# Four rows of the first fourth chunk, loaded through ScalarE's DMA queue

## The chip, the cores and the metric

The kernel runs on one core of a Trainium2 chip. The metric is device time in microseconds (us) of one execution. Without the profiler, three runs of the kernel before took 1325.69, 1326.71 and 1327.58 us; their median, 1326.71 us, is the time before. One execution was profiled, and its trace is what every view below was read from.

## The reference

For two batches, eight heads and rows and columns of 2112, a bias that depends on the clipped distance of row and column is added to the logits, and a softmax is taken over each row:

```python
rel = pos[:, None] - pos[None, :]
rel_clipped = np.clip(rel, -max_rel, max_rel) + max_rel      # max_rel = 16
logits = logits + rel_bias[:, rel_clipped][None, :, :, :]
exp = np.exp(logits - logits.max(axis=-1, keepdims=True))
return (exp / exp.sum(axis=-1, keepdims=True)).astype(np.float32)
```

There are 2 x 8 x 2112 = 33,792 rows of 8,448 bytes. All of them are read once and written once.

## The kernel before, in words

The rows are laid over 128 partitions, 264 consecutive rows to a partition. They are worked off in 44 chunks; a chunk is 6 consecutive rows of every partition (`R = 6`), so 50,688 contiguous bytes in each partition and 6336 KB in all. Four chunks make one pass of the outer loop (`NBUF = 4`, 11 passes), and chunk number m of a pass lives in buffer `X[m]`. There are just these four buffers, so at any time at most four chunks are between the start of their load and the end of their store.

Who does what:

- SyncE issues the loads (`load`, line 89), all on its own DMA queue, which the page lists as q1. At the start it issues chunks 0 to 3 one behind the other (lines 95 and 96). Then it loops: it waits until the store of chunk n has landed (`take` on `st[m]`, line 86) and issues the load of chunk n + 4 into the same buffer.
- VectorE first builds the bias table (lines 118 to 166; the shuffle at line 142 is the first instruction there that needs `rel_bias` in SBUF). In each pass it copies a window of that table (line 170), and for each chunk it waits for the load (`take` on `ld[m]`, line 86), then adds the bias row by row while it takes the maximum (line 184, six instructions), waits for ScalarE's sums, takes their reciprocal (line 208) and scales four of the six rows (line 211).
- ScalarE takes the exponential of each row (line 195), scales the other two rows (line 216), waits until all six rows are scaled, and issues the store (`store`, line 93) on its own DMA queue, which the page lists as q10. Ahead of all that it issues the small load of `rel_bias` (line 120) on the same queue.

So the order of the transfers is set by two queues, each first in first out: SyncE's holds only loads of chunks, ScalarE's holds the small bias load and then only stores. A transfer of a whole chunk is 128 contiguous rows of 50,688 bytes, one for each partition; the 16 DMA engines take 8 of them each. "Row" below, when a DMA is meant, is one of these 50,688-byte rows.

Below, Ln and Sn are the load and the store of chunk n, counted from 0 to 43 over all passes.

Of the kernel before, what the change touches and what calls it, by code (L numbers as in the profile page):

```python
# [15 lines left out]
def kernel(  # L16
# [6 lines left out]
    nc = tc.nc  # L23
    P = 128
    B, H, S, S2 = logits.shape
# [3 lines left out]
    RP = B * H * S // P  # L29
# [4 lines left out]
    NBUF = 4  # L34
    R = 6
# [2 lines left out]
    assert K * G == RP  # L38
    SW = S + G - 1
    DV = 4  # L40

    io = ctx.enter_context(tc.tile_pool(name="io", bufs=1))
    X = [io.tile([P, R * S], FP32, tag=f"X{b}", name=f"X{b}") for b in range(NBUF)]
# [21 lines left out]
    def view(t, offset, dims):  # L65
        return bass.AP(tensor=t.tensor, offset=t.offset + offset, ap=[[list(t.ap[0])[0], P]] + dims)

    def rows(t, k, m):
        return bass.AP(
            tensor=t.tensor, offset=t.offset + m * R * S + k * (G * S), ap=[[RP * S, P], [1, R * S]],  # L70
        )

    with tc.tile_critical(no_gpsimd_drain=True):  # L73
        ld = [nc.alloc_semaphore(f"ld{b}") for b in range(NBUF)]
# [6 lines left out]
        zero = nc.alloc_semaphore("zero")  # L81
        idx = nc.alloc_semaphore("idx")
        dve = nc.alloc_semaphore("dve")

        def take(eng, sem, n):
            eng.wait_ge(sem, n).then_inc(sem, -n)  # L86

        def load(k, m):
            nc.sync.dma_start(out=X[m][:, :], in_=rows(logits, k, m)).then_inc(ld[m], 16)
# [2 lines left out]
            take(nc.scalar, scaled, R)  # L92
            nc.scalar.dma_start(out=rows(out, k, m), in_=X[m][:, :]).then_inc(st[m], 16)

        for m in range(NBUF):
            load(0, m)
        with nc.Fori(0, K - 1, 1, engines=[ENG.SP]) as k:
            for m in range(NBUF):
                take(nc.sync, st[m], 16)
                load(k + 1, m)  # L100
# [3 lines left out]
        v = nc.vector  # L104
# [6 lines left out]
        def settle():  # L111
# [9 lines left out]
            out=bass.AP(tensor=F2.tensor, offset=F2.offset, ap=[[Q * step, P // Q], [1, H * W]]),  # L121
            in_=bass.AP(tensor=rel_bias.tensor, offset=rel_bias.offset, ap=[[0, P // Q], [1, H * W]]),
        ).then_inc(rb, 16)
        nc.gpsimd.iota(pid[:, :], pattern=[[0, 2]], base=0, channel_multiplier=1).then_inc(idx, 1)
        nc.gpsimd.iota(
            num, pattern=[[1, NB + 1]], base=0, channel_multiplier=0,
# [11 lines left out]
        for o, n, s, op in ((eq, NB, q, ALU.is_equal), (lt, NB, q, ALU.is_lt), (hsel, NB, h, ALU.is_equal),  # L138
# [24 lines left out]
                           in_=view(reg, 1, [[1, NB - 1], [0, RP - W]])))  # L163
# [9 lines left out]
        def row(m, i):  # L173
            return X[m][:, i * S : (i + 1) * S]

        def col(t, m, i, n=1):
            c = m * R + i
            return t[:, c : c + n]

        def add(m):  # L180
            take(v, ld[m], 16)
            for i in range(R):
                x = G - 1 - m * R - i
                v.tensor_tensor_reduce(  # L184
                    out=row(m, i), in0=row(m, i), in1=F2[:, x : x + S],
                    scale=-1.0, scalar=BIG, op0=ALU.add, op1=ALU.min, accum_out=col(nmax, m, i),
                ).then_inc(added, 1)
# [12 lines left out]
        def scales_begin(eng, m):  # L200
            if m < NBUF - 1:
                eng.wait_ge(inv, m + 1)
            else:
                take(eng, inv, NBUF)

        def scale(m):
            take(v, expd, R)
            v.reciprocal(out=col(rec, m, 0, R), in_=col(tot, m, 0, R)).then_inc(inv, 1 if m < NBUF - 1 else NBUF + 1)  # L208
            scales_begin(v, m)
            for i in range(DV):  # L210
                v.tensor_scalar_mul(out=row(m, i), in0=row(m, i), scalar1=col(rec, m, i)).then_inc(scaled, 1)  # L211

        def scale_rest(m):
            scales_begin(nc.scalar, m)
            for i in range(DV, R):
                nc.scalar.activation(  # L216
# [3 lines left out]
        with nc.Fori(0, K, 1, engines=[ENG.DVE]) as k:  # L220
            window(k)
            for m in range(NBUF):
                add(m)
                scale(m)
# [36 lines left out]
```

## Time and profile before

| What | Value |
|---|---|
| median of 3 runs without profiler | 1326.71 us |
| profiled execution, its own time | 1327.36 us |
| its span in the trace | 1325.6 us |
| VectorE (DVE) busy | 866.1 us, 65% |
| ScalarE (ACT) busy | 757.2 us, 57% |
| DMA, bytes moved | 570.98 MB |

The span runs from the first to the last thing that the profile records of the execution; 1.8 us of the profiled execution's own time lie outside it. Busy shares are shares of the span. The profile's page gives for each engine the busy time, for the DMA the busy share in 40 equal slices of the span and the GB/s in each, and for each DMA instruction how long after its issue its data had landed. In the view in order of time, a row begins with the start and the duration in us, then engine, line and operation; "SPq" and "ACTq" are the parts of SyncE and ScalarE that issue DMAs and wait on semaphores. What stands in square brackets is the idle time of the engine just before the row, and what ended it. "DVEq L86" there is a wait of VectorE on a semaphore, line 86 being the helper that all such waits go through.

### The profile page before, as it was taken

To read this page: it belongs to the slowest core of one execution; us is meant where nothing else is said; L and a number is where in the kernel's file an instruction comes from. 1 tells how busy PE (TensorE), PEld (TensorE's weight loads), DVE (VectorE), ACT (ScalarE), POOL (GpSimd) and SP (SyncE) were. 2 spreads that over 40 slices of the span, in tenths; PEclk is the share of its full clock that TensorE was granted. 3 is DMA by queue.
4 is the path that set the end of the run, shared out by engine and by line. 5 is a ranking of instruction groups with operands and counts; after the bars stand their busy time and mean duration, and the time that the engine had idled before them with its cause. 6 is when DMAs were issued, how large, how long until landed. Compare 5 with 4: busy or idle time off the path is not lost. (4 is left out here: it accounts for less than half of the span.)

```text
span 1325.6 us, 2109 instructions
## 1 busy us (share of the span) xinstructions
DVE 866.1 (65%) x781; ACT 757.2 (57%) x627; POOL 0.4 (0%) x6
## 2 busy tenths in 40 slices
DVE  6886656566766675566667566556766676566663
ACT  3776555556665565555556565555665665555563
POOL 0000000000000000000000000000000000000000
DMA  9999999999999999999999999999999999999998
GB/s 416 416 433 424 441 428 428 441 424 433 441 428 431 436 425 433 439 430 434 434 430 433 437 434 425 437 434 434 428 439 436 422 441 434 431 431 436 428 433 389
DMA packets 12682, 570.98 MB, mean 431 GB/s; under 512 B 1412, under 2 KB 1416, under 8 KB 1416
## 3 DMA queue, kind: packets, MB, share of 16 engines
q1 hardware_dynamic: 6336, 285.48, 50.1%
q10 hardware_dynamic: 6344, 285.48, 49.8%
q14 instruction: 2, 0.02, 0.0%
HBM read 285.48 MB, written 285.47 MB: 431 GB/s over the span
## 5 line engine op out<-in xcount | busy, mean ns | idle before, releaser
L195 ACT ACTIVATE X<-X,nmax 128x2112 f32<-128x2112 f32 x264 | 542.6, 2055 | 508.0 <-DVE nmax L184 475.3
L184 DVE CUSTOM_DVE_ANT_0 X<-X,F 128x2112 f32<-128x2112 f32 x264 | 605.2, 2354 | 322.3 <-DVEq L86 322.3
L211 DVE TENSOR_SCALAR X<-X,rec 128x2112 f32<-128x2112 f32 x176 | 220.3, 1315 | 2.8
L216 ACT ACTIVATE X<-X,rec 128x2112 f32<-128x2112 f32 x88 | 176.1, 2048 | 17.2 <-DVE rec L208 12.2
L208 DVE RECIPROCAL rec<-tot 128x6 f32<-128x6 f32 x44 | 8.4, 191 | 106.2 <-DVEq L86 106.2
L195 ACT ACTIVATION_READ_ACCUMULATOR X<-X,nmax 128x1 f32 x264 | 49.2, 186 | 0.0
L195 ACT ACT_TABLE_LOAD x11 | 14.1, 1283 | 22.6 <-ACTq L86 19.9
L170 DVE COPY F<-F 128x2135 f32 x11 | 26.1, 2373 | 0.5 <-DVEq L86 0.5
L184 DVE DVE_READ_ACCUMULATOR2_ANT nmax<- 128x1 f32 x264 | 21.7, 82 | 0.0
L142 DVE LOAD_MASK_SELECT F<-F x1 | 0.0, 14 | 6.0 <-DMA F<-in_rel_bias_dram 6.0
L162 DVE COPY F<-own 128x1617 f32<-128x1617 f32 x1 | 1.8, 1835 | 0.0
L118 DVE MEMSET F<- 128x264 f32 x1 | 0.3, 278 | 1.1 <-SPq L73 1.1
L140 DVE TENSOR_SCALAR Z<-rec,Z 128x8 f32<-128x8 f32 (+1 forms) x5 | 0.8, 227 | 0.1
L148 DVE TENSOR_REDUCE own<-F 128x33 f32<-128x264 f32 x1 | 0.6, 608 | 0.1
L161 DVE TENSOR_TENSOR F<-F,own 128x264 f32<-128x264 f32 x1 | 0.4, 442 | 0.1
L145 DVE TENSOR_TENSOR F<-F,Z 128x264 f32<-128x264 f32 x1 | 0.4, 428 | 0.1
L142 DVE STREAM_SHUFFLE F<-F 128x264 f32<-128x264 f32 x1 | 0.4, 443 | 0.0
L158 DVE TENSOR_TENSOR F<-Z,own 128x264 f32<-128x264 f32 x1 | 0.4, 432 | 0.0
L166 DVE COPY F<-own 128x247 f32<-128x247 f32 x1 | 0.4, 410 | 0.0
L164 DVE COPY F<-own 128x247 f32<-128x247 f32 x1 | 0.4, 408 | 0.0
L156 DVE SCALAR_TENSOR_TENSOR own<-Z,own 128x8 f32<-128x8 f32 x1 | 0.2, 227 | 0.2 <-DVEq L86 0.2
L153 DVE TENSOR_SCALAR own<-Z,own 128x8 f32<-128x8 f32 x1 | 0.2, 226 | 0.1
(11 smaller groups left out, 1.6 us busy)
## 6 DMA issues: line engine op xcount, KB each, us to landing
X<-in_logits_dram SPq DMA_DIRECT2D x44, 6336.0 KB, 39.0
out_dram<-X ACTq DMA_DIRECT2D x44, 6336.0 KB, 58.8
F<-in_rel_bias_dram ACTq DMA_DIRECT2D x1, 4.1 KB
```

Source lines behind the costliest of these rows:

```text
L140: then(v.tensor_scalar(out=o, in0=num[:, 0:n], scalar1=s, scalar2=None, op0=op))
L142: then(v.stream_shuffle(out=T, in_=T, mask=[0] * Q))
L145: then(v.tensor_tensor(out=heads, in0=view(F2, 0, [[W, H], [1, W]]), in1=view(hsel, 0, [[1, H], [0, W]]), op=ALU.mult))
L148: then(v.tensor_reduce(out=rbK, in_=view(F2, H * W, [[1, W], [W, H]]), axis=mybir.AxisListType.X, op=ALU.add))
L158: then(v.tensor_tensor(out=bands, in0=view(eq, 0, [[1, NB], [0, W]]), in1=view(rbK, W - 1, [[0, NB], [-1, W]]), op=ALU.mult))
L162: then(v.tensor_copy(out=view(F, C0 + W, [[RP, NB - 1], [1, RP - W]]), in_=view(reg, 1, [[1, NB - 1], [0, RP - W]])))
L170: then(v.tensor_copy(out=F2[:, 0:SW], in_=F[:, bass.ds(RP - G - k * G, SW)]))
L184: v.tensor_tensor_reduce(out=row(m, i), in0=row(m, i), in1=F2[:, x : x + S], scale=-1.0, scalar=BIG, op0=ALU.add, op1=ALU.min, accum_out=c ...
L195: nc.scalar.activation(out=row(m, i), in_=row(m, i), func=ACTF.Exp, scale=-1.0, bias=col(nmax, m, i), accum_out=col(tot, m, i),).then_inc( ...
L208: v.reciprocal(out=col(rec, m, 0, R), in_=col(tot, m, 0, R)).then_inc(inv, 1 if m < NBUF - 1 else NBUF + 1)
L211: v.tensor_scalar_mul(out=row(m, i), in0=row(m, i), scalar1=col(rec, m, i)).then_inc(scaled, 1)
L216: nc.scalar.activation(out=row(m, i), in_=row(m, i), func=ACTF.Copy, scale=col(rec, m, i),).then_inc(scaled, 1)
```

## The change

At the start SyncE now issues chunks 0, 1 and 2 whole, and of chunk 3 only the first two of its six rows. ScalarE issues rows 2 and 3, and then rows 4 and 5, of chunk 3 on its own queue, right behind the bias load and ahead of its first exponential, so ahead of every store. Between the bias load and these two it counts a semaphore up 15 times and takes it down again. All three parts have 128 pieces of 16,896 bytes instead of 128 rows of 50,688. The two parts on ScalarE's queue count up a semaphore `head` of their own, which VectorE waits for ahead of each chunk of buffer 3; it is never taken down, so that after the first pass the wait is met at once. From chunk 4 on everything is issued as before.

```diff
+    GAP = 15
...
+        head = nc.alloc_semaphore("head")
+        gap = nc.alloc_semaphore("gap")
...
-        for m in range(NBUF):
+        def part(eng, m, i, n, sem):
+            src = rows(logits, 0, m)
+            eng.dma_start(
+                out=X[m][:, i * S : (i + n) * S],
+                in_=bass.AP(tensor=src.tensor, offset=src.offset + i * S, ap=[[RP * S, P], [1, n * S]]),
+            ).then_inc(sem, 16)
+
+        for m in range(NBUF - 1):
             load(0, m)
+        part(nc.sync, NBUF - 1, 0, 2, ld[NBUF - 1])
...
+        for _ in range(GAP):
+            nc.scalar.sem_inc(gap, 1)
+        take(nc.scalar, gap, GAP)
+        for i in range(2, R, 2):
+            part(nc.scalar, NBUF - 1, i, 2, head)
...
             take(v, ld[m], 16)
+            if m == NBUF - 1:
+                v.wait_ge(head, 16 * (R // 2 - 1))
```

## The prediction

> **What bounds the kernel now.** I read the page first: busy shares, the slices of the span, the queues, the costliest groups.
>
> ```profile
> span 1325.6 us, 2109 instructions
> DVE 866.1 (65%) x781; ACT 757.2 (57%) x627; POOL 0.4 (0%) x6
> DMA  9999999999999999999999999999999999999998
> DMA packets 12682, 570.98 MB, mean 431 GB/s; under 512 B 1412, under 2 KB 1416, under 8 KB 1416
> q1 hardware_dynamic: 6336, 285.48, 50.1%
> q10 hardware_dynamic: 6344, 285.48, 49.8%
> L184 DVE CUSTOM_DVE_ANT_0 X<-X,F 128x2112 f32<-128x2112 f32 x264 | 605.2, 2354 | 322.3 <-DVEq L86 322.3
> ```
>
> No compute engine is full; VectorE idles 322.3 us ahead of its adds, waiting for loads (DVEq L86). The DMA engines are full in every slice, half of their time for each queue. The next view is the stretches of the span, with DMA share and GB/s as the last two columns.
>
> ```profile
> 17.00:32.00 15.00, 14.06 (x12) 10.41 (x9) 0.00 (x0) 1.00 1.00 433
> 40.00:1300.00 1260.00, 832.93 (x737) 734.49 (x609) 0.00 (x0) 1.00 1.00 433
> 1300.00:1322.00 22.00, 5.20 (x5) 4.56 (x4) 0.00 (x0) 1.00 1.00 433
> ```
>
> 433 GB/s with loads alone (17 to 32), with both queues, and with stores alone at the end. So a second queue adds no rate, and as the bytes stay the same, the time can move only by idle DMA time made or removed. At 433 GB/s the 570.98 MB take 1318.7 us; the span is 1325.6, so **all idle time and latency there is comes to 6.9 us**. The kernel is a loop of four chunks in four buffers around the DMA engines, and what counts is the head, where the loop gets its order, and the tail, where it runs dry. The rows in order of time:
>
> ```profile
> 0.97 2.02 SPq L89 DMA_DIRECT2D X<-in_logits_dram  x4
> 1.40 1.12 ACTq L120 DMA_DIRECT2D F<-in_rel_bias_dram  x1
> 8.74 0.01 DVE L142 LOAD_MASK_SELECT F<-F  x1 [5.99 <-DMA F<-in_rel_bias_dram]
> 18.66 2.36 DVE L184 CUSTOM_DVE_ANT_0 X<-X,F 128x2112 f32<-128x2112 f32 x1 [0.94 <-DVEq L86]
> 40.34 0.38 ACTq L93 DMA_DIRECT2D out_dram<-X  x1
> 75.75 0.34 SPq L89 DMA_DIRECT2D X<-in_logits_dram  x1
> 105.96 0.34 SPq L89 DMA_DIRECT2D X<-in_logits_dram  x1
> 115.08 2.36 DVE L184 CUSTOM_DVE_ANT_0 X<-X,F 128x2112 f32<-128x2112 f32 x1 [6.09 <-DVEq L86]
> ...
> 1245.95 0.33 SPq L89 DMA_DIRECT2D X<-in_logits_dram  x1
> 1276.37 0.34 ACTq L93 DMA_DIRECT2D out_dram<-X  x1
> 1284.53 2.36 DVE L184 CUSTOM_DVE_ANT_0 X<-X,F 128x2112 f32<-128x2112 f32 x1 [8.49 <-DVEq L86]
> 1306.28 0.34 ACTq L93 DMA_DIRECT2D out_dram<-X  x1
> ```
>
> In this order: the four first loads; the bias load; VectorE's start on the bias, on L0, S0's issue, the issues of L4 and L5, VectorE's start on L4; then L43's issue, S42's issue, VectorE's start on L43, S43's issue. S42 to S43 is 29.91 us for one load and one store, 16 rows on each DMA engine: **a row takes 1.87 us, a pair (one of each queue) 3.74, a chunk alone 14.96.**
>
> L4 reaches VectorE 9.1 us after L5 was issued (115.08 - 105.96): when a store lands and frees a buffer, the load before is still 9 us from done. I call this the **lag**. Each queue gets one chunk per 29.9 us, so the lag is carried unchanged from pass to pass, and shows at the end: L43 takes 1284.53 - 1245.95 = 38.6 us, one period and a lag of 8.7. The head sets it.
>
> **The tail.** From VectorE's start on L43 to S43's issue are 21.75 us of compute (1306.28 - 1284.53). Meanwhile the DMA engines live on S41 and S42. Whether they run dry is read from the landing times of each queue's transfers:
>
> ```profile
> DMA to landing us min/median/max: 18.2/58.8/59.5
> DMA to landing us min/median/max: 17.5/39.0/82.6
> ```
>
> The first row is the stores', the second the loads'. The quickest load (L0, on empty queues: 0.97 + 17.5 = 18.5, just ahead of 18.66) took 17.5 us; the quickest store, S43, took 18.2. So S43 waited behind S42 for at least 0.7 us, if its own latency was that of L0, and at most 18.2 - 14.96 = 3.2. I take 1.0, near the lower end, because L0's row is the one like it. **So the tail is covered, by 1.0 us only.** If L43 comes later by x against the stores, S43 is issued x later, while S42 ends only x/2 later (in the extra x both queues still share the engines). The idle time added is x/2 - 1.0.
>
> **The change, part by part.**
>
> *The counting.* 15 increments on ScalarE, behind the bias load's issue that ends at 2.52. The nearest row is of an instruction that only touches semaphores:
>
> ```profile
> L73 SPq EVENT_SEMAPHORE  x3: 17/17/28, 1324.5 to 1324.7; - x3
> ```
>
> 15 x 17 to 28 ns is 0.3 to 0.4 us; were each as long as a DMA issue (0.34), 5.1. ScalarE has nothing to do before 21 us, so it costs nothing itself. I take 0.4: the parts are issued at about 3.0 and 3.4, as L0's second row is starting.
>
> *Two parts on ScalarE's queue.* On each DMA engine they are 16 pieces of a third of a row, 0.62 us each, and two completion marks (the page's 1412 packets under 512 B are such marks, 16 per transfer and 4 for the bias). 10.0 us of DMA time in all. The question is how an engine shares between q1 and q10. The bias load speaks on that: issued by 2.52, its 4.1 KB land only at 8.74. L0 landed by 18.5 and its rows are 1.87 long, so its rows end near 5.4, 7.3 and 9.2 (18.5 less 7, 6 and 5 rows), or up to half a us earlier. A transfer of a few packets has waited for more than one row's end; that fits one turn for its data, another for its mark, and a whole row of q1 between. **I take it that the queues alternate packet by packet, whatever the size.** Then about 7 of the 16 pieces fall between the rest of L0's rows: 7 x 0.62 = 4.4 us. VectorE's start on L0 goes from 18.66 to 23.0, S0's issue from 40.34 to 44.7. The other 9 pieces run beside L1; L1 lands at about 43, and VectorE is busy with chunk 0 until 44.4, which hides it.
>
> *What that does to the lag.* When S0 comes, the ScalarE parts have used 10.0 us of DMA time, but S0 is only 4.4 us later. So q1 is behind by 5.6 us, or **3.0 rows**. The list on q1 has the same number of packets as before, since chunk 3's part there is 8 pieces and a mark in place of 8 rows and a mark. S0's 8 rows and mark go one turn for one turn with it. So when S0 lands and L4 is issued, three more packets stand ahead on q1 than before, and as turns are then taken in pairs of 3.74 us, the lag is 9 + 3 x 3.74 = 20 us.
>
> The walk agrees. S0's first row goes near 47.5 (44.7, 1.0 to the first byte, a row under way). By then the engines have worked since 3.5 (18.5 - 14.96): 44 us, 23.5 rows, 5.3 of them ScalarE's parts, so 18.2 rows of q1. L2 has 5.8 left, each paired with a row of S0: 5.8 x 3.74, to 70. S0's last two rows and its mark pair with pieces at 2.5 us: S0 lands near 76, as now (75.75). The last five pieces and their mark pair with rows of S1, to 91; L4's rows then pair at 3.74, to 121 (now 115), and S1, two rows and a mark short, lands near 98.5 (now 105.9). That is a lag of 22. I go by the count: **L43 lands 11.2 us later after its issue, near 49.8.**
>
> *Mid-run.* Nothing is idle: with the longer lag q1 always holds a load, and S2 is issued near 92, 6 us ahead of S1's end. L2 lands near 71, and VectorE, free of chunk 1 near 66, waits 5 us for it; S0 and S1 keep q10 full meanwhile.
>
> *The third part and `head`.* SyncE's issue of it is one of the same four. VectorE's 11 waits on `head` are met at once, 0.03 us each in 322.3 us of idle time. The two issues more on ScalarE (0.34 each) lie before its first exponential.
>
> *Cost of a piece beyond its bytes.* Not shown directly. Loads alone (17 to 32) and both queues with their marks (40 to 1300) move the same 433 GB/s, rounded to 1; 1 in 433 over 1260 us is 2.9 us for 84 marks per engine, so at most 0.035 us per packet. The change adds 18 packets per engine: 0 to 0.6 us. I take 0.1.
>
> **Sum.** Tail idle 11.2/2 - 1.0 = 4.6, plus 0.1, nothing else: **+4.7 us**. The span goes to 1330.3, the profiled execution's own time from 1327.36 to 1332.1. That execution lies 0.65 above the median; on the median 1326.71 + 4.7 = **1331.4 us**.
>
> Bounds: the cover of 0.7 to 3.2 gives +4.9 to +2.4; one packet more or less in the lag is 1.87 us either way, so +0.5 to +6.8 with both, and with the 0.6 above, +7.4. With the counting at its upper bound the parts come 4.7 us later, two to three of the seven pieces no longer pass L0, and the last ones stand ahead of S0 on q10 instead; q1 is then about two packets behind and not three: +2.8.
>
> **The rivals.**
>
> *No change: the engines share by bytes, or by whole transfers.* The mechanism: the 8 small pieces on q1 let only 5 us of stores pass, not 15, and the ScalarE parts delay L0 by their full 10 us. Then S0 comes 10.0 us later after 10.0 us of extra work, q1 is behind by nothing, its list is 5.3 rows (10.0 us) shorter, and the lag falls below 9: S43 stays covered. If whole transfers take turns, L0 is late by one part at most, 5.0 us, and q1 is behind by 10.0 - 5.0 = 5.0 us, but its list is 10.0 us shorter: the lag falls again. Deciding point: the time of L43 to landing; the tail's cover is gone at 38.6 + 2.0 = 40.6 us, and below that nothing is lost. Price 0 to 0.3, time 1326.8. For it: all 16 engines full at 433 GB/s in every stretch. Against it: the bias load's 8.74. Beside this stands the Trainium skill, page "DMA: Bandwidth & Descriptors": its section "Queues, rings and completion order" says that an engine drains a whole packet, typically 9 to 17 descriptors, from one queue before it switches. By that rule a part of the change would go in one turn, and the sum would be near 0. The bias load's landing speaks against such long turns here. The same page of the Trainium skill says under "Issuing engines are not separate DMA queues" that issuing from several engines saves only issue time, which would also give no change; it does not speak of the order in which transfers land.
>
> *Faster.* The head's lost time goes: the span less 1318.7 leaves 6.9 us, of which S43's latency and the first load's (17.5 - 14.96 = 2.5, and up to 3.2) stay. At most 1.2 us is left: 1325.5. A gain of over 0.2% (2.65 us, about what a measurement of this kernel can tell from no change) would need more than there is.
>
> *Dearer.* The pieces cost their upper bound and the lag grows by four packets: +7.1, 1333.8; the walk's lag of 22, not the count's, points this way.
>
> **How the numbers follow.** The forecast (alternating packets, lag up by three, +2.7 to +6) 0.62; dearer 0.11; no change 0.23, in which I count the parts of the forecast that stay below 2.65; faster 0.04. So slower 0.73, same 0.23, faster 0.04. The forecast's own range is 1329.4 to 1332.7. "No change" has more than 2 in 10, so the range must reach it: from 1326.3 to 1334.5, with some 0.1 left out on each side.
>
> **What would show it right or wrong.** Right: the first add near 23, S0's issue near 44.7, L4's near 76, L5's near 98 (now 105.96); L43 about 50 us from issue to its add; S43 landing in about 17.5, since nothing is ahead of it; and about 4.7 us in which the DMA moves nothing, between S42's end and S43's start. Wrong: the first add near 28 or later and L43 in 40 us or less (sharing by bytes); L0 hardly later than 18.66 (long turns); or idle DMA slices in mid-run, which nothing in the sum allows for.

## The result, and the profile after

The changed kernel takes 1333.64 us (median of 6 runs, 1333.17 to 1334.30), beside 1325.80 us for 6 runs of the kernel before. That is **7.8 us more**, a ratio of 1.0057 with a 95% interval of 1.0044 to 1.0070. In a later set of runs it was 1333.50 beside 1326.77, ratio 1.0032 (1.0010 to 1.0055; there the kernel before itself varied between 1325.5 and 1336.5, which widens the interval). The ratios, here and below, are not those of the two medians; they lie near those of the means, so that long runs of the kernel before count in them. The profiled execution took 1333.18 us. The forecast was 1331.4: the direction and the place are as said, the size is too small by 3 us (4.7 for 7.8). The time lies above the forecast's own 1329.4 to 1332.7, and inside the wider range that ends at 1334.5.

The page of the changed kernel, the lines that answer to those shown of before:

```profile
span 1331.4 us, 2127 instructions
DMA  9999999999999999999999999999999999999996
DMA packets 12970, 570.98 MB, mean 429 GB/s; under 512 B 1444, under 2 KB 1448, under 8 KB 1448
q10 hardware_dynamic: 6632, 289.81, 50.3%
q1 hardware_dynamic: 6336, 281.15, 49.0%
L202 DVE CUSTOM_DVE_ANT_0 X<-X,F 128x2112 f32<-128x2112 f32 x264 | 605.2, 2355 | 329.9 <-DVEq L89 329.9
```

The same bytes, and 288 packets more, which are the 18 per DMA engine that the prediction counted (q1 has 6336 as before). All slices of the DMA row are full but the last, which fell from 8 to 6. The rows in order of time, in the order in which those of before were listed:

```profile
3.74 0.85 ACTq L100 DMA_DIRECT2D X<-in_logits_dram  x2
22.51 2.36 DVE L202 CUSTOM_DVE_ANT_0 X<-X,F 128x2112 f32<-128x2112 f32 x1 [4.71 <-DVEq L89]
44.17 0.38 ACTq L96 DMA_DIRECT2D out_dram<-X  x1
77.34 0.34 SPq L92 DMA_DIRECT2D X<-in_logits_dram  x1
101.00 0.34 SPq L92 DMA_DIRECT2D X<-in_logits_dram  x1
121.96 2.36 DVE L202 CUSTOM_DVE_ANT_0 X<-X,F 128x2112 f32<-128x2112 f32 x1 [5.85 <-DVEq L89]
...
1239.80 0.33 SPq L92 DMA_DIRECT2D X<-in_logits_dram  x1
1292.15 2.36 DVE L202 CUSTOM_DVE_ANT_0 X<-X,F 128x2112 f32<-128x2112 f32 x1 [8.50 <-DVEq L89]
1313.91 0.34 ACTq L96 DMA_DIRECT2D out_dram<-X  x1
```

ScalarE's two parts; VectorE's start on L0, 3.9 us later than before; S0's issue, 3.8 us later; the issues of L4 and L5; VectorE's start on L4. The lag is 121.96 - 101.00 = 21.0 us, where it was 9.1. At the other end L43 takes 1292.15 - 1239.80 = 52.4 us in place of 38.6. What that does is seen in the stretches around the end, DMA share and GB/s last. First the kernel before, then the changed one:

```profile
1300.00:1305.00 5.00, 4.15 (x5) 4.54 (x4) 0.00 (x0) 1.00 1.05 456
1305.00:1309.00 4.00, 1.05 (x1) 0.01 (x1) 0.00 (x0) 1.00 0.91 393
1309.00:1313.00 4.00, 0.00 (x0) 0.00 (x0) 0.00 (x0) 1.00 1.02 444
```

```profile
1300.00:1305.00 5.00, 5.00 (x5) 4.74 (x5) 0.00 (x0) 1.00 0.89 385
1305.00:1309.00 4.00, 1.44 (x4) 3.33 (x5) 0.00 (x0) 1.00 0.12 51
1309.00:1313.00 4.00, 4.00 (x4) 3.64 (x2) 0.00 (x0) 1.00 0.00 0
1313.00:1317.00 4.00, 0.68 (x1) 0.00 (x0) 0.00 (x0) 1.00 0.95 406
```

Before, the DMA engines work through; a share a little over or under 1 comes from packets being booked where they start. In the changed kernel most of them stand idle from 1305 on, while VectorE and ScalarE still work on chunk 43, until S43 is issued at 1313.91. Idle are 0.11 x 5 + 0.88 x 4 + 1.00 x 4 = **8.1 us** up to 1313, in the mean over the 16 engines. The trace's single packet records show the whole stretch. A transfer's 16 completion marks tell when each engine is done with it. In the kernel before, S42's marks lie at 1307.8 in the mean, and S43's first rows go at 1307.8: no gap. In the changed kernel the marks lie at 1305.8 and the rows go at 1314.8: 9.0 us. Mid-run there is no loss: from 95 to 1300 us the DMA moves 434 GB/s. The landing times say the same; the first row is the stores', the second that of SyncE's whole loads:

```profile
DMA to landing us min/median/max: 16.4/45.5/47.7
DMA to landing us min/median/max: 21.4/52.2/68.9
```

S43, the quickest store, lands in 16.4 us now, not 18.2 (17.5 forecast): nothing is ahead of it any more. The stores have become quicker (median 45.5, before 58.8) and the loads slower (52.2, before 39.0) by the same 13 us: four buffers, the same period, only the place where a chunk waits has moved.

The spans differ by 5.8 us, the medians by 7.8. The profiled execution of the kernel before, 1327.36 us, lies 1.6 over the median of its six runs, that of the changed one 0.5 under its own; that is the difference. It shows in the marks, too: S42 ends 2.0 us earlier in the changed kernel's trace.

### The profile page after: what moved, and what is told of

The parts are those of the page before. It is cut to its first block, busy times and chain, and to the rows that moved or that the text cites. A ratio compares the mean times of both kernels' runs of the same rounds, so it can differ in the third digit from the quotient of the medians.

```text
span 1331.4 us, 2127 instructions
## 1 busy us (share of the span) xinstructions
DVE 866.1 (65%) x781; ACT 757.2 (57%) x627; POOL 0.4 (0%) x6
## 3 DMA queue, kind: packets, MB, share of 16 engines
q1 hardware_dynamic: 6336, 281.15, 49.0%
## 5 line engine op out<-in xcount | busy, mean ns | idle before, releaser
L202 DVE DVE_READ_ACCUMULATOR2_ANT nmax<- 128x1 f32 x264 | 21.8, 83 | 0.0
## 6 DMA issues: line engine op xcount, KB each, us to landing
out_dram<-X ACTq DMA_DIRECT2D x44, 6336.0 KB, 45.5
X<-in_logits_dram SPq DMA_DIRECT2D x43, 6336.0 KB, 52.2
```

Source lines behind the costliest of these rows:

```text
L202: v.tensor_tensor_reduce(out=row(m, i), in0=row(m, i), in1=F2[:, x : x + S], scale=-1.0, scalar=BIG, op0=ALU.add, op1=ALU.min, accum_out=c ...
```

## The experiments

The theory on trial: the queues take turns packet by packet, whatever the size; what q1 has left when S0 comes sets the lag; the lag is carried to the end; there it decides whether the DMA engines idle ahead of S43. The rivals: that sharing goes by bytes; that the loads on ScalarE's queue or the late S0 cost by themselves; that the loss lies elsewhere than in the tail. Each ratio is against runs of the kernel before on the same chip.

### Tiny loads in place of the change

The sharpest test leaves the change out. In the kernel before, SyncE issues one load more behind L3 that nobody reads, of 512 bytes for each of n partitions:

```diff
         for m in range(NBUF):
             load(0, m)
+        nc.sync.dma_start(
+            out=tiny[0:n, :],
+            in_=bass.AP(tensor=logits.tensor, offset=logits.offset, ap=[[RP * S, n], [1, 128]]),
+        ).then_inc(tin, 16)
```

With n = 16:

> The kernel before, with one load more on SyncE's queue behind L3: 16 partitions of 512 bytes that nobody reads, so one tiny packet and one mark on each DMA engine; 8 KB, nothing on ScalarE's queue. Theory (a packet takes a turn whatever its size): two turns more on q1 let two more rows of the stores pass, the lag grows by two pairs of 3.74 us: L43 takes 44 to 48 us (38.6 before), time 2 to 6 us over before. Rival 1 (sharing by bytes, or the loss coming from the pieces or from ScalarE's loads): 8 KB change nothing, L43 38 to 40 us, time within 0.5 us.

With n = 32:

> As the run with 16 partitions, with 32: two tiny packets and one mark per DMA engine, 16 KB. Theory: three turns, the same number as in the changed kernel: L43 takes 48 to 53 us, time 5 to 9 us over before, as the changed kernel in the same call. Rival 1: within 0.5 us of before.

With n = 64:

> As before, with 64 partitions: four tiny packets and one mark per DMA engine, 32 KB. Theory: five turns: L43 takes 55 to 60 us, time 8 to 13 us over before; if it comes out far above that, the state in which two parts on SyncE's queue ran 1531 us begins here. Rival 1: within 0.5 us of before.

And the changed kernel on the same chip:

> The changed kernel once more, on the same chip as the three others, for comparison: L43 51 to 53 us, 6 to 9 us over before.

| Run | Turns added on q1 | Lag at L4 (us) | L43, issue to add (us) | Median (us) | Ratio to before |
|---|---|---|---|---|---|
| n = 16, 8 KB | 2 | 16.3 | 47.2 | 1330.18 | 1.0007 (0.9981 to 1.0033) |
| n = 32, 16 KB | 3 | 20.3 | 52.8 | 1331.57 | 1.0021 (0.9996 to 1.0046) |
| changed kernel | | 20.9 | 52.5 | 1333.50 | 1.0032 (1.0010 to 1.0055) |
| n = 64, 32 KB | 5 | 31.9 | 68.1 | 1515.05 | 1.1396 (1.1353 to 1.1439) |

The kernel before had a median of 1326.77 us on this chip. The rows of the run with n = 32: the issue of L5, VectorE's start on L4, the issue of L43, its start on that, and S43's issue.

```profile
100.42 0.34 SPq L91 DMA_DIRECT2D X<-in_logits_dram  x1
120.73 2.36 DVE L191 CUSTOM_DVE_ANT_0 X<-X,F 128x2112 f32<-128x2112 f32 x1 [11.73 <-DVEq L88]
...
1239.64 0.33 SPq L91 DMA_DIRECT2D X<-in_logits_dram  x1
1292.47 2.36 DVE L191 CUSTOM_DVE_ANT_0 X<-X,F 128x2112 f32<-128x2112 f32 x1 [8.81 <-DVEq L88]
1314.22 0.34 ACTq L95 DMA_DIRECT2D out_dram<-X  x1
```

Its tail, DMA share and GB/s last:

```profile
1300.00:1305.00 5.00, 5.00 (x5) 4.74 (x5) 0.00 (x0) 1.00 0.77 335
1305.00:1309.00 4.00, 1.44 (x4) 3.33 (x5) 0.00 (x0) 1.00 0.06 25
1309.00:1313.00 4.00, 4.00 (x4) 3.96 (x2) 0.00 (x0) 1.00 0.00 0
```

Row for row this is the changed kernel: L43 in 52.8 us, most of the DMA idle from 1305 to 1313 (the profiled execution took 1333.57 us, 2 more than the median). 16 KB that nobody reads, on SyncE's queue, with L0 and S0 as early as before (18.79 and 40.46), give the lag and the idle tail of the change. Sharing by bytes cannot do that, nor can anything that needs ScalarE's queue, large pieces or a late S0. The lag follows the count for two turns (+7.2 us) and three (+11.2), at 3.74 each (7.5 and 11.2); five give +22.8, where the count has 18.7. The time is less sharp: L43 came as forecast for n = 16 and 32, but these two medians, +3.4 and +4.8 us, have intervals that reach to no change, the second under the 5 to 9 expected.

With n = 64, L43 took 68.1 us (55 to 60 expected) and 188 us were lost (8 to 13). The expectation names such a jump as possible, since the run with two parts on SyncE's queue, told further down, had been made before; more on it stands at the end.

### Where the loss is: the last store in parts

The head is left as changed. The last chunk alone is added, exponentiated, scaled and stored in three groups of two rows, so that its first store is issued earlier. (The loops over the passes run once less and the last pass is written out.)

```diff
+        def last_dve(m):
+            take(v, ld[m], 16)
+            for i in range(4):
+                last_add(m, i)
+            last_scale(m, 0)
+            last_add(m, 4)
+            last_add(m, 5)
+            last_scale(m, 1)
+            last_scale(m, 2)
```

> The changed kernel, head untouched, with the last chunk worked off in three groups of two rows and stored in three parts, so that its first store is issued about 12 us after its add starts and not 21.75. Theory (the whole loss is DMA time that is idle between S42 and S43, because L43 comes late against the stores): L43 still takes 51 to 53 us, the idle stretch before the last store goes, and the time is 4 to 8 us below the changed kernel, within 3 us of the kernel before. Rival (the loss lies in the head or in the rate with the longer lag, and the tail only shows it): as the changed kernel, 6 to 8 us over before.

Measured: 1329.24 us (11 runs, 1328.12 to 1329.89) beside 1326.34 before, ratio 1.0015 (1.0003 to 1.0027). The rows: VectorE's start on L43 and the first part of S43; then the tail.

```profile
1292.84 2.36 DVE L245 CUSTOM_DVE_ANT_0 X<-X,F 128x2112 f32<-128x2112 f32 x1 [8.59 <-DVEq L89]
...
1304.74 0.34 ACTq L277 DMA_DIRECT2D out_dram<-X  x1
```

```profile
1300.00:1305.00 5.00, 4.96 (x6) 4.09 (x4) 0.00 (x0) 1.00 0.89 385
1305.00:1309.00 4.00, 4.00 (x3) 1.99 (x2) 0.00 (x0) 1.00 0.89 380
1309.00:1313.00 4.00, 3.93 (x7) 2.31 (x4) 0.00 (x0) 1.00 0.61 258
```

L43 is as late as in the changed kernel (52.4 us), but its first rows go 11.9 us after the add starts and not 21.8. From 1300 to 1313 the engines idle 0.11 x 5 + 0.11 x 4 + 0.39 x 4 = 2.6 us in place of 8.1, and of the 7.8 us that the change cost 2.9 are left. So the loss is in the tail, some 5 us of it shown by this run; the rival, which had 6 to 8 us left, is out.

The same last chunk in the kernel before:

> The kernel before with the same last chunk in three parts. Theory: where S42 covers the compute of chunk 43 there is nothing to gain, 0 to 1 us; but in the earlier call some runs of the kernel before were 4 and 10 us longer than its best, and if that is the same idle stretch (the 16 DMA engines apart from one another, so that most end S42 early), those runs come down too and this kernel stays near 1324 to 1327 in all runs. Rival (those long runs are slow all the way through): it varies as the kernel before does.

1326.24 us beside 1326.34, ratio 1.0008 (0.9993 to 1.0023): where S42 covers chunk 43, nothing is gained. The second half of the expectation failed: its 12 runs still include 1329.94, 1330.47 and 1336.32, as those of the kernel before do (up to 1333.92 here). So the long executions of the kernel before are not the idle stretch that this edit shortens; none of them was profiled, and what they are stays open.

### The pieces of the change

ScalarE's four rows in one part:

```diff
-        for i in range(2, R, 2):
-            part(nc.scalar, NBUF - 1, i, 2, head)
+        part(nc.scalar, NBUF - 1, 2, 4, head)
```

> The changed kernel with ScalarE's four rows in one part (8 pieces of 33,792 bytes and one mark per DMA engine in place of 16 of 16,896 and two marks); SyncE's part is as in the change, all parts 128 partitions wide. Theory (turns): seven pieces pass L0, 8.8 us and not 4.4; S0 is issued near 49, but q1 is then behind by 10.0 - 8.8 = 1.2 us only, 0.7 row in place of 3.0: L43 takes 40 to 44 us, time 0 to 3 us over the kernel before, 5 us below the changed kernel. Rival (the later S0, the more is lost): S0 5 us later than in the change, so at least as slow as it.

Measured: 1329.49 us beside 1326.34, ratio 1.0025 (1.0015 to 1.0036). S0's issue, then L43's issue and VectorE's start on it:

```profile
47.79 0.37 ACTq L96 DMA_DIRECT2D out_dram<-X  x1
...
1247.50 0.33 SPq L92 DMA_DIRECT2D X<-in_logits_dram  x1
1292.37 2.36 DVE L201 CUSTOM_DVE_ANT_0 X<-X,F 128x2112 f32<-128x2112 f32 x1 [8.51 <-DVEq L89]
```

S0 is 3.6 us later than in the changed kernel, and yet less is lost in the median: the late S0 is not what costs. The lag fell, but less than counted: L43 takes 44.9 us (40 to 44 expected), and 3.2 us are lost (0 to 3). These rows come from one of the longest of the 12 executions, 1333.41 us, as long as the changed kernel's in spite of the smaller lag. L43's marks lie 9.6 us apart in it, and the next run shows what that does.

The parts issued later, by more increments (`GAP = 60` and `GAP = 150`):

> The changed kernel with 60 increments in place of 15: the parts are issued near 6.8 us, at the 0.071 us per increment that 150 of them took. Theory: about six pieces pass L0, the lag lies between that with 15 (L43 52.3 us) and with 150 (37.4): L43 takes 46 to 50 us, time 3 to 6 us over the kernel before. Rival (only the kind and number of transfers counts): as the changed kernel.

> The changed kernel with 150 increments in place of 15 ahead of ScalarE's two parts; at the 0.08 us that one took in the changed kernel (15 between 2.52 and 3.74) they are issued near 14.7, when L0 is nearly done. Theory (turns): L0 lands near 19, S0 is issued near 41, the pieces run beside L1 and L2 (S0 stands behind the last of them), L43 takes 33 to 37 us, time within 1 us of the kernel before: the sign of the change hangs on how many pieces pass L0. Rival 1 (the pieces themselves, or their place ahead of the stores, cost): 5 us or more over before still. Rival 2 (bytes): no change.

With 150 the parts are issued at 13.12 and hardly pass L0 (first add at 19.56). L43 takes 37.4 us (33 to 37 expected), and the time is 1328.34 beside 1329.62 before on that chip, ratio 0.9994 (0.9961 to 1.0027): no cost that can be told from none, where the change cost 0.57%. With 60 they are issued at 7.33 and L43 takes 45.1 us (46 to 50 expected). So the order of the lags holds (L43 in 52.4, 45.1, 37.4), but the time does not follow it: 1333.98 us, 7.6 over before (3 to 6 expected), ratio 1.0046 (1.0026 to 1.0066), with runs from 1326.85 to 1337.68. The profiled one is among the long ones (1336.67), and its tail shows what else there is:

```profile
1300.00:1305.00 5.00, 5.00 (x7) 4.61 (x7) 0.00 (x0) 1.00 0.80 345
1305.00:1309.00 4.00, 4.00 (x3) 3.87 (x3) 0.00 (x0) 1.00 0.18 76
1309.00:1313.00 4.00, 1.44 (x4) 3.33 (x5) 0.00 (x0) 1.00 0.15 63
1313.00:1317.00 4.00, 4.00 (x4) 3.13 (x2) 0.00 (x0) 1.00 0.09 38
```

A share of 0.18, then 0.15, then 0.09 is three engines of 16, then two, then one or two still on S42 while the others are done. The engines have drifted apart. In the packet records, L43's 16 completion marks lie 13.0 us apart here, 5.9 in the changed kernel, 2.1 in the kernel before. The add starts 0.5 us after L43's last mark in all three, so the compute starts with the slowest engine while the quickest has long ended S42. So the lag alone does not give the time. The stretch from S42's mean mark to S43's first rows goes with it better:

| Profiled execution | Idle stretch (us) | Time (us) |
|---|---|---|
| before | 0.0 | 1327.36 |
| n = 16 | 5.4 | 1329.26 |
| changed | 9.0 | 1333.18 |
| one part | 9.0 | 1333.41 |
| n = 32 | 9.7 | 1333.57 |
| changed, again | 9.6 | 1334.03 |
| `GAP = 60` | 11.6 | 1336.67 |

Why the engines drift is not settled. With 150 increments, the profiled execution took 1339.12 us, though L43's marks lie only 4.6 us apart; S42's lie 14.0 apart, 8.5 us are idle, and S42's mean mark itself comes 4 us later than in the changed kernel. Other runs of that kernel take 1326.

### Three that went astray

Chunk 3 split by partitions, so that one queue has whole rows and the other pieces:

```diff
-        part(nc.sync, NBUF - 1, 0, 2, ld[NBUF - 1])
+        slab(nc.sync, NBUF - 1, 80, 48, 0, R, ld[NBUF - 1])
...
-        for i in range(2, R, 2):
-            part(nc.scalar, NBUF - 1, i, 2, head)
+        for i in range(0, R, 2):
+            slab(nc.scalar, NBUF - 1, 0, 80, i, 2, head)
```

That is whole rows on SyncE's queue (`slab` takes first partition, partitions, first row, rows); the other run has it the other way round.

> The other half: 80 partitions in three parts of two rows on ScalarE's queue (15 pieces and three marks per DMA engine), 48 partitions with whole rows on SyncE's (3 rows and one mark). Theory (turns): S0 is issued near 44, as in the changed kernel; q1 is behind by 2.6 rows for the parts, but its list for chunk 3 has 4 turns in place of 9: L43 takes 31 to 36 us, the tail is covered, time within 1 us of the kernel before. Rival 1 (pieces ahead of the stores on ScalarE's queue, and the late S0, are what costs): as the changed kernel, 6 to 8 us over before. Rival 2 (bytes): no change, so this run does not tell it from the theory.

> Chunk 3 is split by partitions: 80 partitions with whole rows of 50,688 bytes on ScalarE's queue (5 rows per DMA engine, one mark), 48 partitions on SyncE's queue in three parts of two rows (9 pieces of 16,896 bytes and three marks per engine). Theory (turns): L0 lands near 27.5 and S0 is issued near 49.5, 9 us later than before; but that delay equals the work done, so q1 is not behind; its list has 12 turns in place of 9 for chunk 3, so three turns more: L43 takes 50 to 53 us, time 5 to 8 us over the kernel before, as the changed kernel. Rival 1 (late S0 is what costs): S0 is 5 us later than in the changed kernel, so slower than it, 10 us or more over before. Rival 2 (bytes): no change.

L43's times came near the count: 34.5 us (31 to 36) and 48.9 us (50 to 53, just missed). The head did not: S0 was issued at 49.7 us (44 expected) and 68.2 us (49.5). Nor did the times: ratios 1.0163 (1.0114 to 1.0212) and 1.0177 (1.0113 to 1.0242), 22 and 25 us. The stretches of the first of the two show where:

```profile
0.00:30.00 30.00, 11.03 (x24) 1.28 (x1) 0.43 (x6) 1.00 0.97 314
30.00:60.00 30.00, 21.23 (x20) 18.67 (x15) 0.00 (x0) 1.00 0.99 306
60.00:100.00 40.00, 28.54 (x27) 26.69 (x25) 0.00 (x0) 1.00 1.05 347
```

The engines are busy, but at 306 to 347 GB/s; in the packet records many rows take longer than 1.87 us while the loads of 80 or 48 partitions are under way (more at the end). So these two runs say nothing on the price of a lag, and little on its origin, since their heads did not run as the count supposes.

And chunk 3 on SyncE's queue alone, in two parts:

```diff
-        part(nc.sync, NBUF - 1, 0, 2, ld[NBUF - 1])
+        part(nc.sync, NBUF - 1, 0, 3, ld[NBUF - 1])
+        part(nc.sync, NBUF - 1, 3, 3, head)
```

> Chunk 3 goes on SyncE's queue alone, in two parts of three rows (16 pieces of 25,344 bytes and two marks per DMA engine in place of 8 rows and one mark); nothing is added to ScalarE's queue. Theory (the queues take turns packet by packet; the extra turns of small pieces on q1 let the stores get ahead, the lag of the loads grows and stays, and the tail pays): S0 is issued at 40.3 as before and lands early, near 69 to 72, L43 takes 55 to 60 us from issue to its add (38.6 before, 52.3 in the changed kernel), and the time is 8 to 12 us over the kernel before. Rival 1 (the loss comes from the loads on ScalarE's queue, which make L0 and S0 late): within 1 us of the kernel before, since L0 and S0 are as early as there. Rival 2 (sharing by bytes): L43 near 40, at most 1 us slower.

1531.50 us, ratio 1.1513 (1.1459 to 1.1568): slower, with L0 and S0 early, as the theory had it against both rivals, but by 202 us where 8 to 12 were expected. L43 takes 68.9 us (55 to 60 expected), the lag at L4 is 31.8. The run with 64 tiny packets is its twin (68.1 and 31.9).

## Why the prediction was right, and where it was short

- **What bounds the kernel: right.** 434 GB/s in mid-run as before, no compute engine nearer its limit, the whole difference in DMA time that stands idle.
- **Turns by packet: right**, and shown apart from the change by 8 and 16 KB of tiny packets. The bias load was read rightly, though L0's rows end earlier than was worked out: by the packet records the first three end at 4.5, 6.4 and 8.3 us on the quickest engines, not 5.4, 7.3 and 9.2. The bias data go at 6.4, behind the second row, and its mark comes at 8.7, behind the third. The Trainium skill, page "DMA: Bandwidth & Descriptors", section "Queues, rings and completion order", has an engine drain a whole packet of typically 9 to 17 descriptors before it switches. By these runs a turn here is one row, piece or mark: two or three of them more move the lag by 7.2 and 11.2 us. Five move it by 22.8, 4 more than counted, which stays open.
- **The rule that several issuing engines only save issue time** (the Trainium skill, same page, "Issuing engines are not separate DMA queues"): the rate bears it out, 433 and 434 GB/s; the time does not, +7.8 us, since the split decides which transfer lands first.
- **The head: right within a few us.** First add 23.0 forecast, 22.51 measured; S0's issue 44.7 and 44.17; L4's issue 76 and 77.34; L5's 98.5 and 101.00. An increment took 0.08 us, not 0.03, so the parts came at 3.74, not 3.0. Their first piece went at 8.3, and 6.6 pieces passed L0 in the mean over the engines, where 7 were counted.
- **The lag: nearly right.** By the count 20 us, by the walk 22; I went by the count. It was 21.0 at L4, so x = 11.8 where 11.2 was put in. At the end it was 22.5 (52.4 less the period of 29.9), but that goes by L43's last mark, so the slowest engine's delay is in it.
- **The tail's price: the term that was mis-sized.** The sum put 4.6 us of idle time; by the packet records it was 9.0, made up of three parts. From L43's mean mark to S42's are 25.1 us before and 19.2 after: the lag takes 6.0 (11.2/2 = 5.6 was put in). From L43's mean mark to its last, on which the compute waits, are 1.3 us before and 5.0 after: the slowest engine takes 3.6, and the sum has no such term. The cover was 0.6 and not 1.0: S43's first rows could have gone at 1307.2, 0.9 us after their issue as in the changed kernel, and S42's mean mark is at 1307.8. 6.0 + 3.6 - 0.6 = 9.0. So the step that fell short is that the 16 DMA engines were treated as one machine, with one landing of L43 and one end of S42. In the changed kernel 14 engines have L43 by 1286.2, the other two only at 1291.1 and 1291.6; already at L8 the last mark is 4.6 us behind the mean. The second profiled execution of the changed kernel shows the same (19.2 and 5.4). As all engines start S43 together, 1.1 us come back at the end: its last mark is 0.1 us behind the mean, before 1.2. That leaves 7.9, beside 7.8 measured. Why two engines are late is open.
- **The rivals.** Sharing by bytes or by whole transfers, no change: out by the tiny loads. Faster: out. "Dearer", +7.1, comes near the measured size by luck: it has the lag grow by four packets, and 11.8/3.74 is 3.2; it has pieces at their upper price, and the run with 150 increments, which has all of them, shows none (ratio 0.9994, 0.9961 to 1.0027). The late engines are not in it.

## What to carry to other kernels

A loop over a few buffers remembers its start: what each DMA queue holds when the first store comes sets how far loads run behind stores, and if nothing in the loop makes up for it, that is still there a thousand us later, where the last chunk has to be covered. When queues compete, count packets and completion marks, not bytes: here 16 KB more on the load queue moved the lag nearly as far as 4 MB of loads put on the store queue. A cover read at the tail holds for one end of one transfer; with 16 engines that are apart, the slowest starts the compute and the quickest begin to idle.

## What the runs showed of the hardware beside that

**A large lag tips the loop over.** With n = 64 the lag started at 31.9 us, with two parts on SyncE's queue at 31.8, both over the 29.9 of a period; the kernels with a lag of 21.0 and less at L4 did not tip. That the period is the border fits, but no run lies between. For n = 64, the rows are the issue of L5, VectorE's start on L4, L43's issue and VectorE's start on it; then two stretches.

```profile
96.93 0.34 SPq L91 DMA_DIRECT2D X<-in_logits_dram  x1
128.80 2.36 DVE L191 CUSTOM_DVE_ANT_0 X<-X,F 128x2112 f32<-128x2112 f32 x1 [19.93 <-DVEq L88]
...
1405.14 0.33 SPq L91 DMA_DIRECT2D X<-in_logits_dram  x1
1473.22 2.36 DVE L191 CUSTOM_DVE_ANT_0 X<-X,F 128x2112 f32<-128x2112 f32 x1 [12.87 <-DVEq L88]
```

```profile
50.00:100.00 50.00, 41.58 (x38) 38.35 (x33) 0.00 (x0) 1.00 1.01 437
300.00:1400.00 1100.00, 625.08 (x552) 550.72 (x456) 0.00 (x0) 1.00 0.93 378
```

From then on the DMA moves 378 GB/s in place of 433, for the whole run. Part of that is idle time (share 0.93); the rest is rows that take longer, since 0.93 of 433 would be 403: in the packet records a row takes 2.0 us in the mean, not 1.87. The 16 marks of one load lie 6 us apart at L4, 35 at L8 and 48 to 50 from L12 on, more than a whole period, and the engines do not come together again. A chunk then takes 34.4 us in the mean (1405.14 - 96.93 over 38 chunks). 32 KB that nobody reads thus cost 188 us; what makes the rows longer was not tried.

**Beside a load of 80 partitions, other rows took longer.** Before its parts had landed (by 64 us in the run with pieces on ScalarE's queue, by 46 in the other), SyncE's rows of 128 partitions took 2.5 and 3.1 us in the mean from 10 us on, later 1.9. The whole rows of the load of 48 partitions took up to 6.5 us, the stores beside it 2.2. The rate was 306 to 347 GB/s in the first 100 us of the run with pieces on ScalarE's queue, 434 from 130 us on. What slows them was not tried. With 128 partitions, pieces of a third of a row ran at nearly the full rate (427 GB/s from 20 to 44 us in the changed kernel).
